# Main products in uninterrupted runs, and the rotary swap by transfers, in a hybrid decoder step on one core

## The chip, the cores and the metric

The kernel runs on one core of one Trainium2 chip. The metric is the device time of one execution in microseconds. A core has five engines with an instruction stream each: TensorE (PE), VectorE (DVE), ScalarE (ACT), GpSimd (POOL) and SyncE (SP, which issues the transfers here). Every stream is worked off in the order in which it was written when the program was built; where an instruction waits, those behind it on the same engine wait too.

## The reference

One decoder layer works on a prompt of 1024 positions and on 8 single-token samples; the kernel puts the 1032 columns side by side. Cut to the prompt's mixer and the rest of the layer:

```python
qkv, z, xbc, dt_raw = split_mix(rmsnorm(x) @ w_in)
for g, (window, dil) in enumerate(((128, 1), (512, 4), (2048, 16))):
    q, k, v = rope(qkv[g, 0]), rope(qkv[g, 1]), qkv[g, 2]       # 8 heads x 64
    o[g], lse[g] = dilated_window_prompt(q, k, v, dil)           # 128 keys back
attn = sum(softmax(lse)[g] * o[g] for g in range(3))
y, h_new = ssd_chunked(*conv_silu(xbc, dt_raw))                  # 16 heads, chunks of 128
ssm = rmsnorm(y * silu(z))
h = x + rmsnorm(concat(attn, ssm) @ w_out)
out = h + rmsnorm((silu(gate) * up) @ w_ffn_out)                 # gate, up of rmsnorm(h) @ w_ffn_in
```

`rope` rotates the two halves of a head against each other: `x1*cos - x2*sin` and `x2*cos + x1*sin`. All results are f32. The samples read caches of keys and values and write them back shifted by one position.

## The kernel before

**Main products.** Activations lie with features on the 128 partitions and the 1032 positions along the free axis. Each operand of a large product is split into a high and a low part (`wh`/`wl`, `xh`/`xl`), and three of the four products are formed. `unit` (line 167 on, the product itself at line 175) computes a block of 128 output features by a third of the positions (344 columns): 8 blocks of the inner dimension, 3 products each, so 24 products into one PSUM bank. `gemm` loads a weight block (`load_w`) and calls `unit` for the three thirds, each followed by an eviction. Such products are called main products here.

**What runs beside them.** The input projection goes first through the 12 blocks that the SSD branch needs, then through 12 blocks for each of three attention patterns (per head pair one for v, q, k: `do_v`, `do_qk`, then `attend`), then through the 8 blocks of `z`. Side work fills in: the SSD chunks (`ssd`, tiles `xt`, `gb`, `yp`, `yo`, `stp`), the rotation (`do_qk`) and the attention (`attend`). `attend` takes a head pair through 8 rounds j: scores `sps` (for two rounds at once, line 646), mask and maximum by DVE into `sm` (L652), `ngm` (L656), exponential by ACT (L660), transposes `ptp` (L667), a copy to `pt` by DVE or ACT (L671, L673), and the product with v, `nps` (L680). `vtp` (L604) are the transposes of v. `ptp` and `vtp` share a pool of one PSUM bank, which is handed out in program order; `qrp`, `krp`, `vtp` (SBUF), `rawp` and `swpp` have two buffers each.

**Rotation.** `do_qk` gets `rw`, the raw projection, from ACT's evictions (L586). Four ACT copies of 32 partitions (L615) write the halves exchanged into `sw`, POOL multiplies `sw` by the sines (L616), DVE `rw` by the cosines (L617), and DVE adds both into `qr` (L620).

**The merge.** When all three patterns are done, their maxima and sums are stored and read back (`st_d`, `sn`), weights are formed (`wo`, transposed as `wtp`, L842) and 16 steps follow (L850 to L859): load `nt` and the weights `wt`, POOL multiplies (L855), DVE adds twice (L856, L857), ACT and DVE split the sum into `ah` and `al`. There are two buffers of `nt`. The output projection takes the SSD part first (`sh`/`sl`, evicted by DVE into `mix`, L239) and the attention part (`ah`/`al`, weights `wah`/`wal`, L980 and L981) after. Then comes the FFN.

**What sets the order.** A scheduler with a model of the engines puts the instructions into their streams when the program is built. Of those that its model has ready it takes the one with the lowest priority number. `prio(kind)` (line 55) sets that number from one running counter for each kind (line 52): evictions from 1 million, weights from 5, side work from 10, the merge (`late`) from 20, main products from 50. So a main product goes where nothing else is ready. The tables and buffers of the rotation are given back behind the third pattern (`rope.close()`), and the buffers of `z` (`zt`) and of the gate (`yg`) come to lie where they were.

## Time and profile before

| | us |
|---|---|
| median of 3 runs | 1859.24 (1858.23 to 1863.11) |
| profiled execution | 1865.26 |
| its span, first to last instruction | 1863.5 |
| PE busy (matmuls) | 1776.0 (95% of the span) |
| DVE busy | 1141.2 |
| ACT busy | 781.4 |
| POOL busy | 320.0 |

Busy is the union of the times in which an engine works. Matmuls overlap in the pipeline, so a busy PE need not be one at its peak; how far apart the products start tells more. The mean granted TensorE clock is 0.98 of full speed. The span has four parts: the SSD inputs (to about 215 us), the three attention patterns with SSD chunks beside them (to 885 us), the `z` products with the merge (to 1050 us), and the output projection and FFN.

### The profile page before, as it was taken

To read this page: it belongs to the slowest core of one execution; us is meant where nothing else is said; L and a number is where in the kernel's file an instruction comes from. 1 tells how busy PE (TensorE), PEld (TensorE's weight loads), DVE (VectorE), ACT (ScalarE), POOL (GpSimd) and SP (SyncE) were. 2 spreads that over 40 slices of the span, in tenths; PEclk is the share of its full clock that TensorE was granted. 3 is DMA by queue.
4 is the path that set the end of the run, shared out by engine and by line. 5 is a ranking of instruction groups with operands and counts; after the bars stand their busy time and mean duration, and the time that the engine had idled before them with its cause. 6 is when DMAs were issued, how large, how long until landed. Compare 5 with 4: busy or idle time off the path is not lost.

```text
span 1863.5 us, 30669 instructions
## 1 busy us (share of the span) xinstructions
PE 1776.0 (95%) x12183; PEld 1659.1 (89%) x12183; DVE 1141.2 (61%) x2228; ACT 781.4 (42%) x1433; POOL 320.0 (17%) x218
## 2 busy tenths in 40 slices
PE   8999999999998999999878999999999999999995
PEld 6999877888887889988758999999999999999995
DVE  6545666766765454446667499886666666423338
ACT  5533554455554555556333235532222222431133
POOL 0000245444234221123442301000000000000020
PEclk9999999999999999999988999999999999999998
DMA  4322344434334243346566355355545445976686
GB/s 157 135 100 79 97 127 125 128 121 116 114 103 156 90 137 103 123 152 224 171 167 182 101 160 180 110 199 171 176 151 183 167 151 197 351 264 215 207 314 206
DMA packets 135198, 298.59 MB, mean 160 GB/s; under 512 B 18432, under 2 KB 85600, under 8 KB 133648
## 3 DMA queue, kind: packets, MB, share of 16 engines
q1 hardware_dynamic: 135056, 296.64, 48.4%
q8 instruction: 95, 1.56, 0.3%
q14 instruction: 47, 0.39, 0.1%
HBM read 247.49 MB, written 137.10 MB: 206 GB/s over the span
## 4 chain that ended last, share of the span: by engine, by line
PE 37%; DVE 8%; DMA 3%; issue 1%; ACT 1%; POOL 1%; DVEq 0%; SPq 0%; POOLq 0%; ACTq 0%
PE fb L1217 20%; PE g L175 16%; DMA nt<-n_d 1%; PE g L955 1%; DVE xr L1043 1%; POOL nt L855 1%; DVE fl L1058 1%; DVE nacc L1000 1%; DVE mix L1055 0%; DVE nt L856 0%; DVE fac L1341 0%; DMA wr<-in_w_fin 0%; DVE nt L857 0%; DMA out_yT<-fac 0%; DMA wt<-w_d 0%
## 5 line engine op out<-in xcount | busy, mean ns | idle before, releaser
L175 PE MATMUL g<-xh,wh 128*128 128x344 f32 x1344 | 443.6, 330 | 9.3 <-ACT zt L903 5.1
L175 PE MATMUL g<-xl,wh 128*128 128x344 f32 x1344 | 440.3, 328 | 1.5 <-DVE xl L231 1.5
L175 PE MATMUL g<-xh,wl 128*128 128x344 f32 x1344 | 439.2, 327 | 0.5 <-DVE wl L164 0.5
L175 PEld LDWEIGHTS g<-xh,wh 128*128 128x128 f32 x1344 | 255.6, 190 | 19.0 <-ACT zt L903 5.6
L175 PEld LDWEIGHTS g<-xh,wl 128*128 128x128 f32 x1344 | 256.2, 191 | 12.3 <-issue 11.0
L175 PEld LDWEIGHTS g<-xl,wh 128*128 128x128 f32 x1344 | 256.1, 191 | 10.6 <-issue 7.7
L1217 PE MATMUL fb<-fh,wsl 128*128 128x258 f32 x1216 | 222.5, 283 | 0.1
L1217 PEld LDWEIGHTS fb<-fh,wsl 128*128 128x128 f32 x1216 | 188.0, 189 | 0.4 <-DVE fs L1113 0.3
L1217 PE MATMUL fb<-fl,wsl 128*128 128x258 f32 x608 | 171.9, 283 | 0.0
L164 DVE TENSOR_TENSOR wl<-wr,wh 128x1024 fp32r<-128x1024 f32 (+1 forms) x93 | 111.7, 1202 | 80.2 <-ACT wh L163 79.9
L175 PE MATMUL g<-hh,wh 128*128 128x344 f32 x432 | 138.1, 320 | 0.1
L175 PE MATMUL g<-hh,wl 128*128 128x344 f32 x432 | 137.8, 319 | 0.0
L175 PE MATMUL g<-hl,wh 128*128 128x344 f32 x432 | 136.9, 320 | 0.0
L163 ACT CAST wh<-wr 128x1024 fp32r<-128x1024 f32 (+1 forms) x93 | 92.5, 995 | 95.0 <-PE g L175 91.5
L660 ACT ACTIVATE sm<-sm,ngm 128x128 f32<-128x128 f32 (+1 forms) x192 | 84.9, 443 | 106.1 <-DVE ngm L656 102.2
L1300 POOL TENSOR_TENSOR ow<-wr,ow 128x512 fp32r<-128x512 f32 x8 | 10.9, 1395 | 658.8 <-ACT ow L1299 658.8
L616 POOL TENSOR_TENSOR sw<-sw,sin 128x1032 f32<-128x1032 f32 x24 | 72.8, 3032 | 251.0 <-ACT sw L615 187.6
L1217 PEld LDWEIGHTS fb<-fl,wsl 128*128 128x128 f32 x608 | 114.9, 189 | 0.0
L615 ACT COPY sw<-rw 32x1032 f32<-32x1032 f32 x96 | 101.0, 1052 | 1.4
L586 ACT COPY rw<-g 128x344 f32<-128x344 f32 x108 | 47.2, 443 | 111.8 <-PE g L175 71.5
L1221 DVE TENSOR_TENSOR fo<-fp,fb 128x258 f32<-128x258 f32 x152 | 62.8, 420 | 45.4 <-PE fb L1217 43.3
L175 PEld LDWEIGHTS g<-hh,wh 128*128 128x128 f32 x432 | 81.2, 188 | 0.3 <-ACT fac L1284 0.3
(362 smaller groups left out, 3801.2 us busy)
## 6 DMA issues: line engine op xcount, KB each, us to landing
out_skv<-in_cache SPq DMA_DIRECT2D x64, 1023.5 KB, 5.7
wr<-in_w_in SPq DMA_DIRECT2D x56, 512.0 KB, 3.7
out_skv<-in_cache SPq DMA_DIRECT2D x16, 1022.0 KB, 5.6
wr<-in_w_out SPq DMA_DIRECT2D x24, 512.0 KB, 3.7
hr<-hid_d SPq DMA_DIRECT2D x22, 516.0 KB, 6.2
hid_d<-fo SPq DMA_DIRECT2D x38, 258.0 KB, 4.5
wg<-in_w_fin SPq DMA_DIRECT2D x19, 512.0 KB, 4.2
wu<-in_w_fin SPq DMA_DIRECT2D x19, 512.0 KB, 5.1
```

The source lines that it names most:

```text
L163: nc.scalar.copy(wh[:, :cols], wr[:, :cols])
L164: nc.vector.tensor_tensor(out=wl[:, :cols], in0=wr[:, :cols], in1=wh[:, :cols], op=ALU.subtract)
L175: last = nc.tensor.matmul(ps, x[:, ws], y[:, c0:c1], start=(k == 0 and j == 0), stop=(k == n - 1 and j == 2))
L586: return nc.scalar.copy(rw[:, c0:c1], ps)
L615: nc.scalar.copy(sw[q * 32:(q + 1) * 32, 0:T], rw[s * 32:(s + 1) * 32, :])
L616: nc.gpsimd.tensor_tensor(out=sw[:, 0:T], in0=sw[:, 0:T], in1=sin, op=ALU.mult)
L660: nc.scalar.activation(out=sm[:, h, :nk], in_=sm[:, h, :nk], func=AF.Exp, scale=SCALE, bias=ngm[:, g, j, i:i + 1], accum_out=den[:, g, j, ...
L855: nc.gpsimd.tensor_tensor(out=nt, in0=nt, in1=wt, op=ALU.mult)
L955: nc.tensor.matmul(pq[m][c], ws[m][j == 1][:, k * P:(k + 1) * P], (sl if j == 2 else sh)[k][:, CH[c][0]:CH[c][1]], start=(k == 0 and j == ...
L1000: nc.vector.tensor_tensor(out=acc, in0=acc, in1=sq, op=ALU.add)
L1217: nc.tensor.matmul(ps, x[:, ks], y, start=(k == 0 and j == 0), stop=(k == 3 and j == 2))
L1221: return nc.vector.tensor_tensor(out=dst, in0=x, in1=y, op=ALU.add)
```

## The change

A main product gets the priority `main` only where it is the first of a run; the others get the new kind `run`, whose numbers (from 3 million) come before weights and side work. A run has 12 products until the second pattern begins and 24, a whole unit, from then on. In `do_qk` the four copies that exchange the halves become four transfers issued by SP, and the multiplication by the sines goes from POOL to DVE. In `attend` all copies to `pt` are made by ACT.

```diff
--- before.py
+++ after.py
@@ -49,7 +49,7 @@
 
 def trunk(tc, a, o):
     nc = tc.nc
-    ctr = {"evac": 1_000_000, "w": 5_000_000, "side": 10_000_000, "late": 20_000_000, "main": 50_000_000}
+    ctr = {"evac": 1_000_000, "run": 3_000_000, "w": 5_000_000, "side": 10_000_000, "late": 20_000_000, "main": 50_000_000}
 
     @contextmanager
     def prio(kind):
@@ -164,14 +164,17 @@
                 nc.vector.tensor_tensor(out=wl[:, :cols], in0=wr[:, :cols], in1=wh[:, :cols], op=ALU.subtract)
         return wh, wl
 
+    run = [12]
+
     def unit(ps, w, hs, ls, c, ch=CH):
         wh, wl = w
         c0, c1 = ch[c]
         n = len(hs)
-        with prio("main"):
-            for k in range(n):
-                ws = slice(k * P, (k + 1) * P)
-                for j, (x, y) in enumerate(((wh, hs[k]), (wl, hs[k]), (wh, ls[k]))):
+        for k in range(n):
+            ws = slice(k * P, (k + 1) * P)
+            for j, (x, y) in enumerate(((wh, hs[k]), (wl, hs[k]), (wh, ls[k]))):
+
+                with prio("main" if (3 * k + j) % run[0] == 0 else "run"):
                     last = nc.tensor.matmul(ps, x[:, ws], y[:, c0:c1], start=(k == 0 and j == 0),
                                             stop=(k == n - 1 and j == 2))
         return last
@@ -612,8 +615,8 @@
             sw = swpp.tile([P, 3 + T], F32, tag="swp", name="sw")
             for q in range(4):
                 s = q ^ 1
-                nc.scalar.copy(sw[q * 32:(q + 1) * 32, 0:T], rw[s * 32:(s + 1) * 32, :])
-            nc.gpsimd.tensor_tensor(out=sw[:, 0:T], in0=sw[:, 0:T], in1=sin, op=ALU.mult)
+                nc.sync.dma_start(out=sw[q * 32:(q + 1) * 32, 0:T], in_=rw[s * 32:(s + 1) * 32, :])
+            nc.vector.tensor_tensor(out=sw[:, 0:T], in0=sw[:, 0:T], in1=sin, op=ALU.mult)
             nc.vector.tensor_tensor(out=rw, in0=rw, in1=cos, op=ALU.mult)
             qp = krp if which else qrp
             qr = qp.tile([P, S], F32, tag="qr", name="qr")
@@ -667,10 +670,7 @@
                     nc.tensor.transpose(tp[:, q * P:(q + 1) * P], sm[:, h, b * P:(b + 1) * P], ident)
             pt = ptp.tile([P, 4, P], F32, tag="pt", name="pt")
             dst = pt[:, 0:2 * nb].rearrange("p q t -> p (q t)")
-            if j % 2 and j % 4 < 2:
-                nc.scalar.copy(dst, tp[:, :2 * nk])
-            else:
-                nc.vector.tensor_copy(dst, tp[:, :2 * nk])
+            nc.scalar.copy(dst, tp[:, :2 * nk])
             if j % 4 == 0:
                 nps = att_ps("nps")
 
@@ -758,6 +758,7 @@
 
     with prio("side"):
         dec_scores(0)
+    run[0] = 24
     pattern(1)
     with prio("side"):
         dec_scores(1)
```

**PE behind main product 3648.** The main products are counted along PE's stream; this is the end of the eighth unit of `z`. Before, this stood there (`g` is a main product, `pnp` belongs to the samples):

```order
L175 MATMUL g<-xh_119,wl 128x344
L787 MATMUL pnp<-ident,pn_8388 128x32
L787 MATMUL pnp<-ident,pn_8391 128x32
L787 MATMUL pnp<-ident,pn_8394 128x32
L792 MATMUL pnp<-ident,sal 128x32 x2
L680 MATMUL nps<-pt,vt 64x128 x2
L667 MATMUL ptp<-ident,sm 128x128 x2
L646 MATMUL sps<-qr 128x128 x4
L792 MATMUL pnp<-ident,sal 128x32 x4
L175 MATMUL g<-xl_127,wh 128x344
```

Now 29 rows stand there between one main product and the next, with eight groups of `ptp`; these are the ones in the middle:

```order
L680 MATMUL nps<-pt,vt 64x128 x2
L670 MATMUL ptp<-ident,sm 128x128 x2
L649 MATMUL sps<-qr 128x128 x4
L680 MATMUL nps<-pt,vt 64x128 x2
L607 MATMUL vtp<-ident,vp 128x128 x4
L788 MATMUL pnp<-ident,pn_8388 128x32
L788 MATMUL pnp<-ident,pn_8391 128x32
L788 MATMUL pnp<-ident,pn_8394 128x32
L793 MATMUL pnp<-ident,sal 128x32 x6
L607 MATMUL vtp<-ident,vp 128x128 x4
L670 MATMUL ptp<-ident,sm 128x128 x2
L680 MATMUL nps<-pt,vt 64x128 x2
```

Rounds of the third and the fourth head pair, and the transposes of the fourth pair's v, moved here; they stood between main products 3428 and 3640 before.

**SP in the third pattern.** Before, SP issued there the weight loads (`wr`), the outputs of the rotated keys (`out_pk2`) and of v (`out_pv2`), and cache copies (`out_skv`), each of which waits for an eviction:

```order
L148 DMA wr_7866<-in_w_in 128x1024
L627 DMA out_pk2<-qr_7297 128x1024
L690 DMA n_d_339<-nh_6871 128x1024
L129 DMA out_skv0<-in_cache0 16x8128
L594 DMA out_pv2<-rw_7435 128x1024
L148 DMA wr_7969<-in_w_in 128x1024
L129 DMA out_skv0<-in_cache0 16x8128
L148 DMA wr_8065<-in_w_in 128x1024
```

Now the pieces of the swap (`sw`) stand among them, for q and k of the third head pair:

```order
L690 DMA n_d_339<-nh_6871 128x1024
L148 DMA wr_8751<-in_w_in 128x1024
L618 DMA sw_7624<-rw_7538 32x1032 x4
L618 DMA sw_7720<-rw_7634 32x1032 x2
L129 DMA out_skv1<-in_cache1 16x16352
L618 DMA sw_7720<-rw_7634 32x1032 x2
L597 DMA out_pv2<-rw_7865 128x1024
L148 DMA wr_8841<-in_w_in 128x1024
```

One cache copy came to stand between the two halves of a swap.

**DVE at the end of the merge.** `nt_8614` and `nt_8624` are the last two of the 16 steps, `mix4` to `mix7` the output blocks whose SSD part DVE evicts. Before:

```order
L239 TENSOR_TENSOR mix4_9531<-g_9773,rt_8748 128x344
L856 TENSOR_TENSOR nt_8614<-nt_8614 128x256
L857 TENSOR_TENSOR nt_8614<-nt_8614 128x256
L859 TENSOR_TENSOR al_8436<-nt_8614,ah_8435 128x256
L239 TENSOR_TENSOR mix4_9531<-g_9799,rt_8748 128x344
L856 TENSOR_TENSOR nt_8624<-nt_8624 128x256
L164 TENSOR_TENSOR wl_9885<-wr_9883,wh_9884 128x1024
L857 TENSOR_TENSOR nt_8624<-nt_8624 128x256
L859 TENSOR_TENSOR al_8436<-nt_8624,ah_8435 128x256
L239 TENSOR_TENSOR mix5_9532<-g_9831,rt_8748 128x344
```

Now:

```order
L857 TENSOR_TENSOR nt_8614<-nt_8614 128x256
L858 TENSOR_TENSOR nt_8614<-nt_8614 128x256
L242 TENSOR_TENSOR mix6_9533<-g_9889,rt_8748 128x344
L860 TENSOR_TENSOR al_8436<-nt_8614,ah_8435 128x256
L857 TENSOR_TENSOR nt_8624<-nt_8624 128x256
L858 TENSOR_TENSOR nt_8624<-nt_8624 128x256
L860 TENSOR_TENSOR al_8436<-nt_8624,ah_8435 128x256
L242 TENSOR_TENSOR mix6_9533<-g_9915,rt_8748 128x344
L242 TENSOR_TENSOR mix7_9534<-g_9947,rt_8748 128x344
```

The last steps moved back by about one and a half output blocks of 48 main products each.

## Rows read from the trace of the kernel before

**Rows 1.** Busy time by stage: window, us, engines busy (instructions), PE clock, DMA share, GB/s.
```profile
215.00:590.00 375.00, 361.55 (x2553) 308.31 (x2552) 254.03 (x597) 198.39 (x411) 151.31 (x107) 0.99 0.39 119
...
885.00:1050.00 165.00, 141.04 (x772) 125.03 (x771) 108.82 (x137) 54.88 (x79) 64.26 (x38) 0.92 0.59 162
1050.00:1863.50 813.50, 787.35 (x5714) 782.71 (x5712) 514.69 (x910) 266.87 (x425) 26.12 (x14) 0.98 0.58 198
```

**Rows 2.** Waits of PE, 215 to 700 us: who, for whom, us, times, longest.
```profile
PE sps L646 <- DVE qr L620: 10.7, 4, 5.4
PE xt L497 <- DMA xg<-xs_d: 7.7, 4, 2.4
PE g L175 <- ACT rw L586: 3.5, 6, 1.3
```

**Rows 3.** Time line of PE around one visit: start us, us, instruction, count.
```profile
308.09 0.31 PE L175 MATMUL g<-xh,wl 128*128 128x344 f32 x1
308.33 0.66 PE L680 MATMUL nps<-pt,vt 128*64 128x128 f32 x8
308.92 0.66 PE L667 MATMUL ptp<-ident,sm 128*128 128x128 f32 x4
309.33 0.41 PE L175 MATMUL g<-xl,wh 128*128 128x344 f32 x1
309.57 0.33 PE L175 MATMUL g<-xh,wh 128*128 128x344 f32 x1
309.74 0.32 PE L175 MATMUL g<-xh,wl 128*128 128x344 f32 x1
```

**Rows 4.** The same around the last round of attention.
```profile
889.57 0.44 PE L680 MATMUL nps<-pt,vt 128*64 128x128 f32 x4
889.93 0.44 PE L667 MATMUL ptp<-ident,sm 128*128 128x128 f32 x2
```

**Rows 5.** Groups by line, 215 to 885 us: busy us, mean ns, idle before it.
```profile
L615 ACT COPY sw<-rw 32x1032 f32<-32x1032 f32 x92 | 96.8, 1052 | 1.4
L616 POOL TENSOR_TENSOR sw<-sw,sin 128x1032 f32<-128x1032 f32 x23 | 70.4, 3059 | 195.6 <-ACT sw L615 132.2 <-PE ptp L667 25.4 <-PE g L175 24.7
...
L652 DVE CUSTOM_DVE_ANT_0 sm<-sps,mask 128x128 f32<-128x128 f32 (+1 forms) x192 | 59.4, 357 | 34.9 <-PE ptp L667 26.3 <-PE sps L646 8.0 <-ACT nh L688 0.3
...
L617 DVE TENSOR_TENSOR rw<-rw,cos 128x1032 f32<-128x1032 f32 x23 | 37.4, 1627 | 18.6 <-ACT sw L615 18.6
```

**Rows 6.** DMA issues, 215 to 880 us: count, KB each, median us to landing.
```profile
out_pv<-rw SPq DMA_DIRECT2D x4, 512.0 KB, 5.8
...
out_pv<-rw SPq DMA_DIRECT2D x3, 64.0 KB, 1.6
```

**Rows 7.** Time line of ACT in a round of the third pattern.
```profile
876.93 0.40 ACT L660 ACTIVATE sm<-sm,ngm 128x128 f32<-128x128 f32 x1
...
877.62 0.19 ACT L660 ACTIVATION_READ_ACCUMULATOR sm<-sm,ngm 128x1 f32 x1
880.44 0.37 ACT L671 COPY pt<-ptp 128x256 f32<-128x256 f32 x1 [2.63 <-PE ptp L667]
```

**Rows 8.** Busy time by stage, a stretch in which PE waits.
```profile
970.00:980.00 10.00, 6.33 (x19) 5.16 (x20) 7.22 (x7) 6.26 (x9) 4.87 (x3) 0.58 0.43 107
```

**Rows 9.** POOL's merge multiply, L855: idle before it (us, times), until what.
```profile
  DMA nt<-n_d: 51.8, 9
```

**Rows 10.** Tile `ah`: duration ns min/median/max, first and last start.
```profile
L175 PE MATMUL g<-ah,wah x48: 314/320/323, 1051.1 to 1128.0; 128*128 128x344 f32 x48
...
L859 DVE TENSOR_TENSOR al<-nt,ah x16: 410/422/1900, 935.8 to 1035.9; 128x256 fp32r<-128x256 f32 x16
```

**Rows 11.** Tile `wah`: the split of the attention part's weights.
```profile
L981 POOL TENSOR_TENSOR wal<-wr,wah x2: 2421/2428/2434, 1040.0 to 1047.2; 128x1024 fp32r<-128x1024 f32 x2
```

**Rows 12.** Waits of SP's queue, 215 to 880 us: us, times, longest.
```profile
SPq L148 <- DVE wl L164: 96.0, 23, 17.8
SPq L129 <- ACT rw L586: 77.1, 10, 13.8
```

## The prediction, made before the changed kernel ran

> **What bounds the kernel now.** The table above has PE busy for 95% of the span, but a share over the whole span says little, so I read the busy times by stage first [rows 1]. From 1050 us to the end (output projection and FFN) PE is busy 787 of 813 us, and nothing in the change is aimed there. From 215 to 590 us (the first two attention patterns beside the SSD chunks) it is busy 362 of 375 us. From 885 to 1050 us, where the patterns are merged beside the `z` products, it loses most: 141 of 165 us at a granted clock of 0.92. So there are two questions: do products and attention pass PE faster or slower before 885 us, and does the end of attention, from which the merge starts, come earlier or later? Second, the waits of PE between 215 and 700 us [rows 2] name three things worth having: scores that wait for the rotated `qr` (10.7 us), SSD transposes that wait for a load (7.7 us), and products that wait for an eviction by ACT (3.5 us). Third, PE's time line around one visit to attention work [rows 3] gives the price that the regrouping is to save.
>
> **Part 1: fewer visits.** Counted in the order up to the first FFN product of the blocked kind (`fb`), main products stand in 212 uninterrupted runs before and in 133 now, nearly all of 12, 24 or 48, so 79 visits to side work go. One visit costs, by [rows 3]: the step from a product to `nps` takes 0.24 us (308.09 to 308.33) where one product follows another after about 0.16, so 0.08 going in; the first product after it takes 0.24 again (309.33 to 309.57), 0.08 coming out; `ptp` to product adds nothing to the 0.41 us of the four transposes. That is 0.16 x 79 = 13 us saved. But the side work is the same and now stands in longer pieces: changes from one kind of side product straight to another rise from 220 to 288. Eight `nps` take 0.59 us until `ptp` starts [rows 3], four take 0.36 [rows 4]: 0.06 for each, so 0.12 is the change, and 68 x 0.12 = 8 us are given back. With changes to and from `sps`, which no row here isolates, it may be twice that. The net lies between -6 and +4 us; I take -3. The regrouping as such is nearly free of gain: what goes at the border between products and side work comes back between the kinds of side work.
>
> **Part 2: the rotary swap.** 96 ACT copies of 1.05 us go (92 of them in this stretch, 96.8 us), and so do 24 POOL multiplies of 3.06 us. DVE takes the multiply, at the price of its twin with the cosines, 1.63 us [rows 5], and gives its 72 `pt` copies to ACT. For each tile the chain from `rw` to the sum was 4 x 1.05 + 3.06 = 7.3 us and becomes a transfer plus 1.6 us. No transfer from SBUF to SBUF stands in the trace. The nearest rows write SBUF to memory: 64 KB of `rw` land 1.6 us after issue, 512 KB after 5.8 [rows 6]. A piece here is 129 KB, and four are issued in turn, so 2.5 to 7 us; I take 3.3, near the 64 KB row. The chain is then 4.9 us, 2.4 shorter (bounds: 3.2 shorter, 1.3 longer). ACT and POOL hold up PE in this stretch only through `qr` and `rw`, so their relief is worth at most what PE waited for those two, 14.2 us, and with the loads 21.9 [rows 2]. Of the four `qr` waits about 7 us go if each shortens by 2.4; with a little for the other two I take 9 us saved, bounds 0 and 20.
>
> **Part 3: attention falls behind the products.** The order shows this, the short description doesn't. A run once started outranks side work, so side work gets one gap per 24 products, where the 212 runs before left one per about 13 in this stretch, and a gap carries mostly one round of attention. A pattern has 36 units and 32 rounds, and the `vtp` and scores need gaps too, so attention just fails to keep up. In the order the scores of the last head pair first appear behind product 3648 instead of 3520, and the last `nps` of attention behind 3816 instead of 3736. Those 80 products, 0.16 us each, are done before the end of attention instead of behind it: +12.8 us for that end.
>
> The lag has a second price. At product 3648 the `z` products must stop, since their buffers lie where `rawp`, `swpp` and the tables lay, and those are free only when the last `vtp` has read `vp`; `vtp` shares one PSUM bank with `ptp` in program order, so it stands behind every round of the third head pair. Where two pieces of side work stood there, 8 rounds stand now, with `vtp` in their middle and no product between them; behind product 3288 there are four. With the smaller places, 11 more rounds than before have no product beside them. What does such a round cost? PE's own work in it I put at 0.9 us: 0.36 for `nps`, 0.2 for two transposes, and half a group of scores. ACT cannot do a round faster than two exponentials (876.93 to 877.81) and a copy of 0.37, 1.25 us [rows 7]; a round with nothing overlapped adds two masks on DVE of 0.36 us [rows 5] and PE's 0.9, some 3 us. So PE idles 0.35 to 2.1 us for each round; as two can overlap I take 1.1, 12 us in all. Add 3 us (0 to 6) for an SSD chain that now stands alone behind product 2280, and 3 us (0 to 6) of slow clock: +18 us, bounds 4 and 35.
>
> On the clock: from 970 to 980 us, where PE waits for side chains, the granted clock is 0.58, a mix of 2.4 and 1.2 GHz [rows 8], against 0.99 from 215 to 590 us with its many short visits [rows 1]. The Trainium skill (TensorE: Matmul & The Clock Gate, section Loop structure matters more than you think) says that a loop nest which keeps the products dense keeps the clock up, and that long waits between them lose it; the trace agrees, with its 0.58. By that rule longer runs help; by [rows 1] the clock before 590 us leaves them 1% to win, and the stretch behind 3648 is one of the kind that loses it.
>
> **Part 4: the merge.** It is a chain of 16 steps, whose `nt` loads wait for one of two buffers; POOL waits 51.8 us for them [rows 9]. It starts from the end of attention and ends with the `al` that starts at 1035.9; the first product on `ah` starts at 1051.1 [rows 10]. Behind the chain only a weight load and its split are needed: `wal` starts at 1040.0 and takes 2.4 us [rows 11], so 1042.4 would do, which leaves 8.6 us of slack. In DVE's order six SSD evictions stood between the chain's end and the products on `ah`, worth the 15 us from 1035.9 to 1051.1; now there are three, about 7.5 us, hardly more than the 6.5 that load and split take. The slack is used up, so the first product on `ah` moves by what the end of attention moves, less 8.6 us. Bounds: all of it (0), or 25 us less, if transfers and DVE are freer because more products are done already.
>
> **The sum**, against the profiled execution's own 1865.26 us: +12.8 (products ahead) - 3 (visits) + 18 (rounds alone) - 9 (shorter waits) = +18.8 at the end of attention; - 8.6 (slack) = +10.2 at the first product on `ah`. From there both programs are bound by PE, and it stays. The profiled execution lies 6.0 us above the median of 1859.24; on the median I forecast 1869 us. What a measurement of this kernel can tell from no change is 0.3%, 5.6 us.
>
> **Rivals.**
> *Longer runs pay (faster).* The place is the stretch from 215 to 885 us. If rounds alone overlap down to ACT's pace (5 us in all), the visits save their most and nearly all waits of [rows 2] go, the end of attention moves by 12.8 - 6 + 5 - 20 = -8; less the slack's 8.6 and with 2 us of clock lost that is -15, so 1844 us. For it: ACT loses up to 74 us of work (101 less 72 x 0.37), POOL 73, and the waits of [rows 2] are real. It decides where a round alone leaves PE idle for less than 0.5 us. Against it: the swap's transfers start from SP's queue.
> *SP's queue holds the swap (much slower).* SP works in order, and it stood still for weight buffers 96.0 us in 23 times, up to 17.8, and behind cache copies that wait for an eviction 77.1 us in 10, up to 13.8 [rows 12]. A swap behind such a row makes `qr` late, and PE waits in front of `sps`. In the third pattern a cache copy stands between two halves of a swap. Two such waits of 10 us over the forecast: 1889 us. Against it: a weight load and the swap of an earlier tile become ready at nearly the same time.
> *It comes out even.* The copies and multiplies that go lay beside PE, the runs were 13 long already, and the slack of the merge takes the lag: 12.8 - 3 + 10 - 12 - 8.6 = -1, so 1858 us.
>
> **How the numbers follow.** The forecast has 0.42, the held swap 0.12, even 0.20, faster 0.26. Slower by over 0.3%: 0.12 and all but 0.02 of the 0.42, so 0.52. Faster by over 0.3%: 0.26 and 0.01 of the even case's spread, 0.27; no change 0.21. The range is 1842 to 1896 us: it holds the faster case and the held swap, and leaves out that several bounds meet, as a merge 25 us quicker with all waits gone, or 35 us of rounds alone behind a held swap. The forecast's own range is 1858 to 1882.
>
> **What would show it.** Right: one stretch of 15 to 20 us between 860 and 910 us in which no main product runs, PE waits in front of `ptp`, `nps` and `vtp`, and the clock falls; few waits for `qr` before 700 us; `wtp` 15 to 25 us later; the first product on `ah` near 1061 us. Wrong: that stretch with PE busy throughout; products before 590 us clearly denser than 0.16 us; `sps` that waits for `sw` transfers over 5 us a time; or a merge over in much less than its 100 us.

## The result, and the profile of the changed kernel

The changed kernel is slower: 1905.07 us median of 4 runs (1904.16 to 1914.37), against 1861.17 us for the kernel before beside it. The ratio is 1.0231, with a 95% interval of 1.0201 to 1.0260. The direction was forecast; the size, +10, was not: it is +44 us on the medians, and the time lies outside the range. The profiled execution took 1914.37 us with a span of 1912.6, 49.1 over the span before, so the sums below are a few us larger than the medians say.

The stages of the changed kernel (window, us, busy time of PE, PEld, DVE, ACT and POOL with their instructions, granted clock, DMA share, GB/s) answer to [rows 1]:

```profile
215.00:590.00 375.00, 352.43 (x2389) 302.91 (x2388) 225.89 (x534) 149.81 (x365) 106.62 (x86) 0.95 0.43 127
...
885.00:1050.00 165.00, 139.39 (x776) 117.76 (x776) 103.88 (x183) 76.21 (x144) 63.56 (x37) 0.88 0.57 172
1050.00:1912.60 862.60, 824.86 (x5917) 817.86 (x5915) 536.52 (x942) 275.53 (x438) 43.13 (x23) 0.98 0.58 195
```

The first two of these rows have a lower clock than before (0.95 for 0.99, 0.88 for 0.92), and everything behind them is late. The waits of PE from 215 to 700 us (us, times, longest), against [rows 2]:

```profile
PE g L178 <- ACT rw L589: 16.9, 9, 3.7
PE xt L500 <- DMA xg<-xs_d: 6.6, 2, 4.1
PE sps L649 <- DVE mx L655: 3.6, 2, 2.8
PE nps L680 <- ACT pt L673: 2.1, 4, 0.7
```

The waits for `qr` are gone, as forecast. A new one stands in their place: a main product that waits for ACT to evict `rw`, 16.9 us where it was 3.5. From 700 us to the last `nps` of attention the changed kernel has these, and the one before, up to its own last `nps` at 894 us, the two behind:

```profile
PE stp L754 <- DVE scs L750: 6.5, 1, 6.5
PE nps L680 <- ACT pt L673: 6.3, 9, 1.6
PE sps L649 <- DVE mx L655: 4.0, 5, 1.5
```
```profile
PE stp L754 <- DVE scs L750: 1.1, 1, 1.1
PE pnp L787 <- DVE pn L786: 1.1, 1, 1.1
```

Behind main product 3648 the changed kernel does what the order said, but for 32 us (891.3 to 923.9 without a main product). The time line of PE there (start, us, instruction, count, idle before it):

```profile
891.27 0.31 PE L178 MATMUL g<-xl,wh 128*128 128x344 f32 x1
...
892.25 0.72 PE L649 MATMUL sps<-qr 64*128 64x128 f32 x8
894.37 0.44 PE L680 MATMUL nps<-pt,vt 128*64 128x128 f32 x4 [1.41 <-ACT pt L673]
894.74 0.44 PE L670 MATMUL ptp<-ident,sm 128*128 128x128 f32 x2
901.68 0.61 PE L754 MATMUL stp<-ident,scs 128*32 128x128 f32 x2 [6.50 <-DVE scs L750]
```

and the same place by windows, then the kernel before over its own last rounds of attention:

```profile
889.00:896.40 7.40, 4.77 (x37) 3.62 (x35) 4.67 (x9) 2.78 (x8) 3.25 (x2) 1.00 0.53 182
896.40:927.10 30.70, 20.86 (x95) 14.36 (x96) 13.56 (x59) 14.70 (x49) 5.17 (x4) 0.50 0.49 183
927.10:940.00 12.90, 12.90 (x89) 11.85 (x88) 8.85 (x12) 9.30 (x15) 6.72 (x5) 1.00 0.58 193
```
```profile
860.00:894.00 34.00, 32.93 (x217) 29.21 (x218) 22.38 (x59) 21.38 (x47) 9.54 (x6) 0.95 0.53 182
```

For 30.7 us the granted clock is 0.50, the lower level of 1.2 GHz, in one piece. It comes back only where main products run again, 3.2 us after the first of them. It fell at 896.4, 1.2 us after the long wait for `scs` had begun. Before, rounds of attention lay between main products, at 0.95, with PE busy 97%.

The later stations, against [rows 10] and [rows 11]:

```profile
L178 PE MATMUL g<-ah,wah x48: 313/320/488, 1093.0 to 1174.9; 128*128 128x344 f32 x48
...
L860 DVE TENSOR_TENSOR al<-nt,ah x16: 360/424/1858, 991.7 to 1091.4; 128x256 fp32r<-128x256 f32 x16
```
```profile
L982 POOL TENSOR_TENSOR wal<-wr,wah x2: 2340/2370/2400, 1091.9 to 1094.3; 128x1024 fp32r<-128x1024 f32 x2
```

The merge still takes 100 us (991.7 to 1091.4) and starts 55.9 later; the first product on `ah` comes 41.9 later (1093.0 for 1051.1).

### The profile page after: what moved, and what is told of

It reads as the page before. It is cut to its first block, busy times and chain, and to the rows that moved or that the text cites. A ratio compares the mean times of both kernels' runs of the same rounds, so it can differ in the third digit from the quotient of the medians.

```text
span 1912.6 us, 30770 instructions
## 1 busy us (share of the span) xinstructions
PE 1799.8 (94%) x12183; PEld 1680.1 (88%) x12183; DVE 1109.2 (58%) x2180; ACT 709.9 (37%) x1411; POOL 250.8 (13%) x194
## 5 line engine op out<-in xcount | busy, mean ns | idle before, releaser
L178 PE MATMUL g<-xh,wh 128*128 128x344 f32 x1344 | 450.9, 336 | 22.2 <-ACT rw L589 16.9
L178 PEld LDWEIGHTS g<-xh,wh 128*128 128x128 f32 x1344 | 259.5, 193 | 41.8 <-ACT rw L589 20.7
L178 PEld LDWEIGHTS g<-xh,wl 128*128 128x128 f32 x1344 | 260.1, 194 | 1.6 <-DVE wl L164 0.8
L655 DVE CUSTOM_DVE_ANT_0 sm<-sps,mask 128x128 f32<-128x128 f32 (+1 forms) x192 | 59.9, 347 | 83.1 <-PE ptp L670 48.5
L1301 POOL TENSOR_TENSOR ow<-wr,ow 128x512 fp32r<-128x512 f32 x8 | 10.1, 1291 | 657.6 <-ACT ow L1300 657.6
L1222 DVE TENSOR_TENSOR fo<-fp,fb 128x258 f32<-128x258 f32 x152 | 63.0, 421 | 49.1 <-PE fb L1218 45.2
L178 PEld LDWEIGHTS g<-hh,wl 128*128 128x128 f32 x432 | 81.2, 188 | 0.0
```

Of the source, the lines that this page charges most:

```text
L178: last = nc.tensor.matmul(ps, x[:, ws], y[:, c0:c1], start=(k == 0 and j == 0), stop=(k == n - 1 and j == 2))
L655: nc.vector.tensor_tensor_reduce(out=sm[:, h, :nk], in0=sps[h][:, c0:c0 + nk], in1=msk, scale=1.0, scalar=0.0, op0=ALU.add, op1=ALU.max, a ...
L1222: return nc.vector.tensor_tensor(out=dst, in0=x, in1=y, op=ALU.add)
L1301: nc.gpsimd.tensor_tensor(out=wl, in0=src, in1=wh, op=ALU.subtract)
```

## The experiments

Times are medians beside runs of the kernel before on the same chip. "Behind" is ratio less 1, times the median before (1861 to 1866 us). The stations come from each kernel's profile: the last `nps` of attention, the main products started by then, the time at half clock up to then, the last `al`, the first product on `ah`. Two traces of one order differ too: up to product 3600 the order on PE of one kernel below (`e18_nostp`) is that of the changed kernel, and its profile reaches that product 7.6 us earlier. Differences of stations between kernels are good to some 8 us.

| kernel | ratio (95%) | behind, us | last `nps` | products | half clock | last `al` | first on `ah` |
|---|---|---|---|---|---|---|---|
| before | 1 | 0 | 894.1 | 3736 | 23.9 | 1035.9 | 1051.1 |
| runs (e1) | 1.0253 (1.0234 to 1.0271) | +47 | 936.2 | 3792 | 71.7 | 1080.4 | 1095.8 |
| swap (e2) | 1.0049 (1.0033 to 1.0066) | +9 | 912.0 | 3781 | 30.7 | 1050.4 | 1058.6 |
| pt (e3) | 1.0127 (1.0108 to 1.0147) | +24 | 910.2 | 3812 | 20.5 | 1054.1 | 1068.7 |
| runs, pt (e4) | 1.0359 (1.0339 to 1.0379) | +67 | 977.3 | 3864 | 109.2 | 1114.9 | 1116.5 |
| swap, pt (e5) | 1.0032 (1.0018 to 1.0047) | +6 | 899.0 | 3736 | 23.9 | 1041.2 | 1056.3 |
| runs, swap (e11) | 1.0195 (1.0169 to 1.0220) | +36 | 923.3 | 3792 | 54.6 | 1068.0 | 1083.1 |
| all three (changed) | 1.0231 (1.0201 to 1.0260) | +43 | 955.9 | 3816 | 92.2 | 1091.4 | 1093.0 |
| runs, patterns 1 and 2 (e9) | 1.0000 (0.9985 to 1.0015) | 0 | 909.3 | 3794 | 27.3 | 1043.8 | 1047.2 |
| runs of 12 throughout (e8) | 1.0158 (1.0126 to 1.0189) | +29 | 935.5 | 3828 | 64.9 | 1074.2 | 1075.8 |
| runs from 2784 on (e12) | 1.0171 (1.0147 to 1.0195) | +32 | 918.3 | 3792 | 44.4 | 1066.4 | 1081.5 |
| runs up to 3216 (e13) | 1.0190 (1.0167 to 1.0212) | +35 | 926.6 | 3806 | 51.2 | 1066.4 | 1080.5 |

### The three edits, alone and together

**Runs alone**, `e1_runs`: before, with the new kind and `run` only.

```
-        with prio("main"):
-            for k in range(n):
+        for k in range(n):
...
+                with prio("main" if (3 * k + j) % run[0] == 0 else "run"):
...
+    run[0] = 24
     pattern(1)
```


> Only the grouping of main products is changed (runs of 12 in the first pattern, 24 from the second on); the rotary swap and the pt copies are those of before. Its trace has the place behind main product 3648 at which nothing but side work stands (6 rounds, 19 pieces; after: 8 and 25; before: none).
> Theory R (the runs are the loss: attention falls behind, and what then stands alone runs at half clock): most of after's loss comes back, +25 to +45 us, 1886 to 1906 us; a stretch of 15 to 30 us at half clock near 890 us.
> Theory S (the swap by transfer is the loss: DVE, in order, waits for it, and ACT's evictions wait behind): between -5 and +10 us, 1856 to 1871 us, with a short piece at half clock near 890 us.
> The rival 'longer runs pay' as put in the prediction: -10 us or better.

Measured: 1911.50 us (1908.14 to 1914.37). Theory R, a little above its range.

**Swap alone**, `e2_swap`:

```
-                nc.scalar.copy(sw[q * 32:(q + 1) * 32, 0:T], rw[s * 32:(s + 1) * 32, :])
-            nc.gpsimd.tensor_tensor(out=sw[:, 0:T], in0=sw[:, 0:T], in1=sin, op=ALU.mult)
+                nc.sync.dma_start(out=sw[q * 32:(q + 1) * 32, 0:T], in_=rw[s * 32:(s + 1) * 32, :])
+            nc.vector.tensor_tensor(out=sw[:, 0:T], in0=sw[:, 0:T], in1=sin, op=ALU.mult)
```


> Only the rotary swap is changed: four transfers from SP's queue in place of ACT's four copies, the multiply by the sines on DVE in place of POOL. Main products lie as before (209 runs up to the first blocked product, 212 before).
> Theory S: DVE waits for sw some 60 us in all as in after, the cache copies' evictions behind it make PE wait; +15 to +35 us, 1876 to 1896 us.
> Theory R: the swap costs little or gains the few us that I had put on it: -9 to +6 us, 1852 to 1867 us, although DVE waits, since PE has enough other work.
> Theory P (the pt copies on ACT are the loss): as R here.

Measured: 1873.56 us (1868.70 to 1878.82), between the two theories.

**pt alone**, `e3_pt`: the branch goes and `nc.scalar.copy(dst, tp[:, :2 * nk])` stays.

> Only the pt copies are changed: all on ACT, where before a quarter were. ACT keeps the 96 swap copies too, so it has 72 more copies of 0.37 us, 27 us of work, and DVE is freed of as much.
> Theory P (pt in ACT's order, behind exponentials and evictions that wait, is a good part of the loss): +10 to +25 us, 1871 to 1886 us, PE waits for pt in front of nps over 10 us in all.
> Theories R and S: within 5 us of before, 1856 to 1866 us, since ACT has room.

Measured: 1889.06 us (1883.61 to 1890.38): nearly Theory P's number (3 us above its range), for a part to which the prediction had given no term. But Theory P's mechanism is not there. It wanted over 10 us of waits for `pt`, and the trace up to the last `nps` has

```profile
PE nps L677 <- ACT pt L670: 2.0, 1, 2.0
```

All waits of PE from 215 us up to there grow only from 28.3 to 34.0 us. What grows is the number of main products ahead of the end of attention: 3812, 76 more than before. At the 0.157 us from one main product to the next these are 12 of the 16.1 us by which attention ends later; the last `al` and the first product on `ah` come 18 us later. That the order is the cause is read from these counts; no run tests it alone.

**Runs and pt**, `e4_noswap`: the changed kernel with ACT's copies and POOL's multiply put back.

> The change without its swap: runs of 12 and 24 and all pt copies on ACT; ACT swaps and POOL multiplies as before. Behind main product 3648 eight rounds stand alone, behind 3072 and 3288 four and three.
> Theory S: close to before, -5 to +12 us (1856 to 1873 us): the loss goes with the swap.
> Theory R: close to after, +30 to +45 us (1891 to 1906 us).
> If the two add up, each about half: +15 to +25 us.

Measured: 1930.05 us (1929.00 to 1935.78). Neither theory has it: without the swap the changed kernel would be 24 us slower still. **Swap and pt**, `e5_noruns`, put `with prio("main")` back around the unit:

> The change without its runs: swap by transfers with the sines on DVE, all pt copies on ACT, main products in the order of before. Alone the swap cost 10 us and the pt copies 26.
> Theory A (ACT's order is what pt fills and the swap empties: each edit undoes the other): +5 to +12 us, 1868 to 1876 us, so that the runs alone make up the rest of after's 43.9.
> Theory B (the two add up, and only the runs make the swap pay): +30 to +38 us, 1893 to 1902 us.

Measured: 1871.47 us (1869.23 to 1876.99). Theory A: beside each other the two cost 6 us, less than either alone. **Runs and swap**, `e11_nopt`, put the branch of the copies back:

> The change without its pt copies: runs of 12 and 24, swap by transfers with the sines on DVE, three quarters of the pt copies on DVE as before. Behind main product 3648 seven rounds stand alone, behind 3072 four.
> Theory A (the runs are worth some 48 us, and swap and pt cancel as far as ACT's order is concerned): without pt the swap's own 10 us come on top of the runs, +45 to +60 us, 1908 to 1924 us.
> Theory B (with the runs in place the swap saves 22 us, as it does beside pt): +22 to +32 us, 1885 to 1896 us.

Measured: 1902.26 us (1898.81 to 1905.09), a little above Theory B. In the three kernels with runs and another edit the loss of the runs shows; swap and pt move it by -11 to +20.

### Where the runs lose

**Runs in the first two patterns only**, `e9_runs_p01`: e1 with one line more.

```
+    run[0] = 1
     pattern(2)
```


> Only the grouping, and only in the first two patterns (12, then 24); in the third the products stand as before, one at a time. No place behind 3648 where side work stands alone.
> Theory L (the loss is what the lag makes at the end: the rounds alone behind 3072 and 3648, their waits and their half clock): 0 to +12 us, 1863 to 1876 us, since main products of the first two patterns passed no later at product 2448 (+2 us) in the run with runs throughout.
> Theory D (long runs lose all along, by the waits at their ends and the clock that falls behind them): +20 to +35 us, 1884 to 1899 us.

Measured: 1866.30 us (1860.45 to 1868.74), before beside it 1866.37: the low end of Theory L. 212 uninterrupted runs became 173 up to the first `fb`, with nothing won and nothing lost. Its largest wait of PE from 215 to 700 us is the new one, longer than in the changed kernel although the swap is the old one:

```profile
PE g L178 <- ACT rw L589: 24.5, 10, 7.7
```

So it is the runs that bring this wait (a unit reaches its PSUM bank before ACT has evicted it), in exchange for those of [rows 2], 21.9 us. **Runs of 12 throughout**, `e8_runs12`, are e1 without `run[0] = 24`:

> Only the grouping, runs of 12 throughout (no step to 24). Behind 3648 five rounds stand alone (6 with 24), behind 3072 none (4 with 24).
> Theory L: the stretch behind 3072 does not come (worth 14 us in the run with 24) and that behind 3648 stays: +20 to +36 us, 1884 to 1900 us.
> Theory 24 (the step to 24 is the whole loss): within 8 us of before, 1856 to 1872 us.
> Theory D: as with 24, less a few us, +38 to +46 us.

Measured: 1895.21 us (1892.43 to 1898.91). Theory L. **Runs of 24 from product 2784 on**, `e12_third`, count the products in `unit`:

```
+        run = 24 if m0 >= 2784 else 1
```


> Only the grouping, and only from main product 2784 on, the third pattern and the z products (runs of 24); the first two patterns as before. Behind 3648 the same 6 rounds stand alone as with runs throughout, behind 3072 none.
> Theory L (what stands alone behind 3648 and what follows from it is the loss): +24 to +36 us, 1888 to 1900 us, like runs of 12 throughout, which have that place too.
> Theory C (the loss needs the long runs of all three patterns, their lag added up): within 10 us of before, 1856 to 1876 us.

Measured: 1895.88 us (1895.00 to 1899.94). Theory L: the third pattern alone is enough, with no lag from the first two. **Runs of 12 and 24 up to product 3216**, `e13_catch`:

```
+        run = 12 if m0 < 1920 else 24 if m0 < 3216 else 1
```


> Only the grouping: runs of 12, of 24 from product 1920 on, and from 3216 on, two thirds through the third pattern, one product at a time as before, so that attention catches up. Five rounds stand alone behind 3072, none behind 3648.
> Theory L: the loss behind 3648 (21 to 26 us in the runs that have it) is gone, that behind 3072 (about 14 us) stays but the slack behind attention's end takes it: 0 to +14 us, 1863 to 1878 us.
> Theory D' (long runs lose wherever they stand in the third pattern): half of the 47 us, +20 to +28 us, 1884 to 1892 us.

Measured: 1899.94 us (1899.01 to 1901.85). A miss for Theory L and worse than Theory D'. There is no place alone behind 3648, and still attention ends 32.5 us later than before, with 70 products more ahead of it. Its five rounds behind product 3072 look like those behind 3648 in small:

```profile
735.00:754.00 19.00, 16.06 (x122) 13.19 (x120) 5.21 (x24) 9.30 (x17) 0.00 (x0) 1.00 0.30 88
754.00:764.20 10.20, 7.10 (x30) 5.07 (x31) 5.88 (x16) 7.39 (x20) 3.42 (x1) 0.50 0.01 2
```

Product 3168 comes 12.6 us later than before, 3744 19.4, 4032 17.8 and 4320 29.5. So bunched rounds cost wherever in the third pattern they stand, and no slack took it up.

**The change with the third pattern as before**, `e14_third1`: the same line as in e9, put into the changed kernel.

> The change with one line more: from the third pattern on one product at a time, as before. Runs of 12 and 24 in the first two, swap by transfers, sines on DVE, pt copies on ACT. No place behind 3648.
> Theory L: the runs cost nothing then; what is left is the +6 us of swap and pt together: 0 to +8 us, 1863 to 1872 us.
> Theory S (the swap's waits on DVE cost by themselves beside the runs): +15 to +25 us.

Measured: 1881.54 us (1879.03 to 1884.60), ratio 1.0090 (1.0069 to 1.0111), +17. The line takes 26 us off the changed kernel. The 17 left are Theory S's number and more than e9 and e5 together (6), so there is a second loss, for which the third pattern's runs are not needed. Where the two lie shows in the starts of main products, in us later than before:

| kernel | 2880 | 3600 | 3648 | 3744 | last `nps` |
|---|---|---|---|---|---|
| runs (e1) | 2.2 | 8.2 | 26.2 | 30.9 | 42.1 |
| runs, patterns 1 and 2 (e9) | 7.1 | 8.1 | 3.5 | 4.1 | 15.2 |
| all three (changed) | 21.4 | 22.0 | 47.6 | 47.9 | 61.8 |
| the same, third pattern as before (e14) | 16.8 | 18.2 | 16.0 | 15.7 | 19.7 |

Of the changed kernel's 47.9 us at product 3744, 21.4 are there at product 2880, ahead of any place with rounds alone in the third pattern, and 25.6 come between 3600 and 3648, where e14 has none. Up to product 2880 the changed kernel has 54.6 us at half clock, e14 44.4, the kernel before 20.5. The early loss stands where runs and pt come together: at product 2880 e4 (runs, pt) is 15.8 us late, e5 (swap, pt) 5.3, and e11 (runs, swap) 8.2 early. With e4 late and no transfer in it, the swap's waits, Theory S's reason, can't be needed for it; what does it is not shown. **A candidate**, `e15_p01_swap`: e9 with the swap by transfers, its multiply left on POOL.

> A candidate: runs of 12 and 24 in the first two patterns only, swap by transfers, but the multiply by the sines stays on POOL and the pt copies stay as before. The last transposes of attention stand behind product 3706 (before 3713, the runs in two patterns alone 3771).
> If it is the multiply on DVE (in order, waiting for the transfer) that made the swap cost 10 us alone: -12 to -3 us, 1851 to 1860 us. If the transfers themselves cost: +4 to +10 us, 1867 to 1873 us.

Measured: 1906.96 us (1903.02 to 1909.54), ratio 1.0224 (1.0202 to 1.0246), +42: outside both. An early end of attention in the order (3706) is worth nothing if PE cannot run the order: 20 us are lost between products 2448 and 2592, and `nps` waits 18.3 us for `pt` up to the end of attention. Those copies stand in DVE's order behind decode sums that wait for POOL (40.0 us in all, up to 9.7) and behind cosines that wait until the transfers have read `rw` (40.3, up to 5.8).

### What slows the rounds that stand alone

**No wait for the decode scores**, `e18_nostp`: the changed kernel with

```
-            nc.tensor.transpose(stp[:32, h * P:(h + 1) * P], scs[:, h]..., ident)
+            nc.tensor.transpose(stp[:32, h * P:(h + 1) * P], ident[:, 0:32] if g == 2 else scs[:, h]..., ident)
```


> The changed kernel, but the last two transposes of decode scores read the identity in place of the scores, so that they wait for nothing (what is left out: the decode scores of the third pattern). In the changed kernel PE waits 6.5 us there, and from that wait on the clock is at half for 30.7 us, over 12 rounds or parts of rounds with PE busy 73 to 83%.
> Theory W (the wait brings the clock down, and the side work behind it runs at half speed for that reason): the stretch keeps full clock or loses it for under 10 us; 6.5 us of wait and about 8 of clock come back, -10 to -18 us against after, 1887 to 1896 us.
> Theory T (rounds without main products are too thin for full clock): the clock falls all the same, for 20 us or more; -2 to -7 us, 1898 to 1903 us.

Measured: 1902.49 us (1897.79 to 1904.47), ratio 1.0209 (1.0192 to 1.0226). By the time Theory T; but the edit did not do what it was for. A wait for another decode tile came in its place, and the clock fell within that one (at 891.9; the wait ended at 892.2), for 27.3 us:

```profile
PE pnp L788 <- DVE pn L787: 4.6, 1, 4.6
```

**Four transposes for one**, `e20_dup`, on top of it:

```
+                    for _ in range(4 if g == 2 and hp >= 2 else 1):
```


> As e18_nostp, and each transpose of the exponentials in the last two head pairs of the third pattern is issued four times (same data, same place): 96 more than needed in 16 rounds and 0.1 us each at full clock, some 10 us more work for PE.
> Theory T (the clock follows how dense PE's work is in the rounds): less time at half clock behind 3648 than in e18_nostp, by 10 us or more, and the time the same as there or up to 5 us less although PE has 10 us more to do.
> Theory W, or a clock that does not respond: the extra work shows, +4 to +12 us against e18_nostp.

Measured: 1910.51 us (1907.51 to 1917.00), 8 us over e18, as the clock that does not respond would have it. Here the wait for `pn` shrank to 0.4 us. The waits of PE from 884 to 927 us, and windows around the stretch at half clock:

```profile
PE sps L649 <- DVE mx L655: 3.1, 3, 2.1
PE nps L681 <- ACT pt L674: 1.4, 2, 0.8
```
```profile
892.00:899.10 7.10, 5.91 (x42) 5.22 (x42) 4.35 (x20) 3.54 (x13) 2.58 (x2) 1.00 0.34 104
899.10:926.40 27.30, 24.43 (x113) 18.61 (x113) 13.09 (x38) 11.29 (x34) 5.77 (x6) 0.50 0.74 266
926.40:937.00 10.60, 10.60 (x74) 9.81 (x73) 5.93 (x14) 8.63 (x17) 3.43 (x3) 1.00 0.18 63
```

The longest wait there is 2.1 us, and that at 887; the clock fell all the same, for 27.3 us, and PE is busy 89% of it, at half speed. So it takes no long wait, which speaks against Theory W, and making PE's work denser with transposes did not hold the clock, against what Theory T expected. It is one profile, but the changed kernel has a smaller place of the kind: behind product 3288 four rounds stand alone, and the clock falls at 821.3 for 6.8 us with no wait over 0.7 us before it. In `e6_pool` it falls 0.2 us ahead of a wait of 3.9 us, and in the six others with a long stretch within a wait of 4.4 to 6.5 us. In e12 the stretch at half clock behind 3648 is 23.9 us; in e9, where main products lie between the rounds, there is none:

```profile
865.50:889.40 23.90, 19.09 (x83) 13.46 (x84) 12.46 (x51) 12.45 (x41) 7.47 (x5) 0.50 0.68 249
```
```profile
893.00:912.00 19.00, 19.00 (x128) 17.46 (x127) 11.84 (x24) 10.48 (x20) 9.55 (x6) 1.00 0.40 118
```

One kernel departs from this. In e11, with seven rounds alone behind 3648, the clock came back between two pieces, 10.7 us before the next main product, and fell again:

```profile
870.40:880.60 10.20, 7.55 (x38) 4.71 (x37) 5.47 (x17) 4.14 (x16) 5.18 (x5) 0.50 0.65 196
880.60:884.10 3.50, 0.80 (x5) 0.31 (x3) 0.69 (x1) 0.58 (x1) 1.70 (x2) 0.99 0.96 306
884.10:894.30 10.20, 7.76 (x35) 5.65 (x35) 7.49 (x27) 5.94 (x18) 2.17 (x2) 0.50 0.94 365
```

What brings the clock down in such a stretch, and what brings it back, stays open.

### What the swap costs

`e10_swap_pool` is e2 with the multiply left on POOL, `e6_pool` the changed kernel with the same.

> The kernel before with only the copies of the swap turned into transfers; the multiply by the sines stays on POOL, so DVE has no more to do than before. With the multiply on DVE the swap cost 10 us alone.
> Theory DVE (the multiply waits for the transfer in DVE's order and holds what is behind it): within 4 us of before, 1859 to 1868 us.
> Theory transfer (four issues on SP and a landing of 2.3 to 7.5 us make qr late in any case): +8 to +20 us, 1871 to 1884 us, since the multiply on POOL is slower by 1.8 us.

> The changed kernel, but the multiply by the sines stays on POOL.
> Theory DVE: -5 to -12 us against after, 1893 to 1900 us.
> Theory transfer: +2 to +15 us against after, 1907 to 1920 us.

Measured: 1887.72 us (1884.15 to 1891.96), ratio 1.0127 (1.0104 to 1.0150), +24; and 1907.22 us (1904.62 to 1912.27), 1.0234 (1.0212 to 1.0256), no different from the changed kernel and at the low end of Theory transfer. In e10 Theory DVE is refuted: alone, the multiply on DVE is the good half of the edit (e2 loses 9 us, e10 24), the transfer the bad one. Beside runs and pt it makes no difference where the multiply stands. Its chain by tile, from the start of the first piece to the start of the sum, is 8.1 us (median of 24) before, 9.3 in e2, 10.1 in the changed kernel and 10.4 in e10. Issues of the changed kernel (count, KB, median us to landing), and its multiplies of 215 to 885 us (busy us, mean ns, idle before):

```profile
sw<-rw SPq DMA_DIRECT2D x96, 129.0 KB, 2.5
```
```profile
L619 DVE TENSOR_TENSOR sw<-sw,sin 128x1032 f32<-128x1032 f32 x23 | 28.4, 1235 | 66.8 <-DMA sw<-rw 63.8 <-DMA kt<-in_cache 2.3 <-DMA y_d<-xg 0.8
```

## Why the prediction was wrong, step by step

I set every step of PE from one product's start to the next, from 215 us to the last `nps`, against the median of the same pair at full clock in the trace before. What is over by more than 0.45 us I count as a wait, the rest as clock if the clock was at half, and otherwise as visits. Against the trace before, in us:

| term | forecast | runs alone (e1) | changed kernel |
|---|---|---|---|
| work ahead of attention's end at full clock (main products) | +12.8 | +12.0 | +17.6 |
| visits | -3 | -5.7 | -7.0 |
| waits (rounds alone 12, SSD chain 3, shorter waits -9) | +6 | +22.8 | +28.4 |
| slow clock | +3 | +14.0 | +23.5 |
| end of attention | +18.8 | +42.1 | +61.8 |
| slack of the merge | -8.6 | +2.6 | -19.9 |
| behind the first product on `ah` | 0 | +4.4 | +7.1 |
| span | +10.2 | +49.1 | +49.1 |

The columns leave under 1.5 us open. How much goes to which row depends on which steps count as the same pair: by tile or by tile and shape, slow clock in the changed kernel comes out between 22 and 27 us and waits between 28 and 33. By count alone the main products are 80 x 0.157 = 12.6 us there and 56 x 0.157 = 8.8 in e1, less than the first row has. So the rows give sizes, not single us; the table of product starts above needs no pairing.

**Part 1, visits: right in kind.** Gone are 79 visits, and they are worth little; the -7.0 lies just beyond the bound of -6. e9 shows a kernel with 39 fewer visits and no time won.

**Part 3, the lag: mechanism right, two sizes wrong.** The 80 products are there (3816 for 3736). The term that failed here is "3 us (0 to 6) of slow clock": it is some 23.5. The prediction named the stretch behind 3648 as one of the kind that loses the clock, but gave the 3 us no working. Time at half clock up to the last `nps` is 92.2 us where it was 23.9; the stretch behind 3648 has 30.7 of it, and 34.1 of the 68.3 more lie ahead of product 2880, where the sum had 3 us for an SSD chain and otherwise only gains. And the price of a round alone, 2.0 us from PE's 0.9 plus 1.1 idle, was taken at full clock: from `nps` to the next transposes PE takes 0.37 us at full clock and 0.63 at half. The waits of the lag were sized well: 12 and 3 forecast, and the profile's rows from 700 us on grow from 3.6 to 21.2 us in all.

That the stretch would stand alone only behind 3648 and 3288 was right; that the long decode chain ends in it was not seen: each of 8 steps loads, multiplies on POOL and sums on DVE, and `stp` waits 6.5 us for the last. What this wait is worth by itself is not shown, since in e18 another of 4.6 us took its place.

**Part 2, the swap and the waits: wrong in sign.** The term "9 (shorter waits)" failed, and with it "I take 3.3, near the 64 KB row": the four issues take some 0.6 us each on SP, and a piece lands 2.5 us after its issue, so the fastest multiply starts 4.2 us after the first issue, and the median one 5.9 to 7.2. The chain became longer by 1 to 2 us, not 2.4 shorter. Hence DVE waits for `sw`, with everything behind it in its order:

```profile
DVE sw L619 <- DMA sw<-rw: 66.6, 21, 12.7
```

The -9 for shorter waits is +6.5 by the rows of 215 to 700 us (24.7 before, 31.2 after, all groups), since the runs put the wait for `rw` where those for `qr` stood; with the clock, PE is 21.4 us late at product 2880. What I had not seen is that the swap is worth something else in company: alone it costs 9 us, but beside runs and pt it saves 24 (e4 to the changed kernel), beside pt 18, beside the runs 11. That its worth changes with the other edits is shown. That ACT's load is the reason is argued, and it can't be all, for the runs give ACT nothing more to do.

The pt copies got no term in the sum and cost 24 us alone, by the counts mostly through the order that the scheduler then chose.

**Part 4, the slack: right in kind, read from the wrong rows.** The 15 us between the last `al` and the first product on `ah` were not DVE's six evictions but the second weight pair. `wah` is made twice, and I had taken only the first: `wal` at 1040.0 and 2.4 us behind it, where [rows 11] have a second at 1047.2. From its end to the first product on `ah` are 1.5 us, not 8.6. Before, the first of three loads of the row below is issued at 1035.1 and the second pair's at 1042.5, when the split of the first has ended and given a load buffer back; its own split ends at 1049.6. In the changed kernel both are issued by 1081, ahead of the last `al`, and only the splits are left:

```profile
L978 SPq DMA_DIRECT2D wr<-in_w_out x3: 367/368/368, 1035.1 to 1043.5; - x3
```
```profile
L979 SPq DMA_DIRECT2D wr<-in_w_out x2: 378/489/600, 1074.4 to 1080.6; - x2
```

From the last `al` to the first product on `ah` are 15.2 us before, 1.6 in the changed kernel, 3.4 in e9 and 15.4 in e1. Where the second pair comes early, the first product on `ah` moves 17 to 20 us less than attention's end (e8, e4, e9, the changed kernel): e9 ends attention 15 us later and loses nothing. In the changed kernel part of it is given back: the second split ends 3.6 us after the first product on `ah`, PE waits 2.9 us for it, and 5.4 of the 7.1 us behind that product arise within the next 80 main products.

Of the rivals, "longer runs pay" is refuted by the result, and in e9, where the runs stand without the stretch, they pay nothing. "It comes out even" falls with the result too. "SP's queue holds the swap" is not the main thing, for the runs lose 47 us without the swap. Of the signs that were to prove the forecast, the stretch of 15 to 20 us without main products was 32, and `wtp`, expected 15 to 25 us later, came 62.8 later (974.9 for 912.1). The direction was right, but a good part of the loss came from places for which the prediction had a gain.

What stays open: why runs and pt together lose 16 to 21 us up to product 2880 (e4, e14, the changed kernel), why e13 loses 35 (12.6 by product 3168 with the bunched rounds, and 70 products ahead of attention's end are 11 by count), and why e15 loses 42. Their losses are located, their causes only in part.

## What to carry to other kernels

Side work that is kept waiting is not saved up for free: where it must be done before the next main products can start, it runs alone, and here mostly at half clock; price a round that would stand alone with PE's part at that clock (0.63 us where 0.37 stood). Look for the buffers or banks at which the main stream must stop, and count what side work stands in front of that point before and after a change of priority. And price an edit that moves work between engines in the company it will have: the swap was +9 us alone and -24 beside two other edits.

## What the runs showed of the hardware that was not expected

Nine of these kernels have five to eight rounds of side work alone behind 3648. In eight of them the granted clock fell to 0.50 there, for 23.9 to 30.7 us in one piece, and rose 0.3 to 6.2 us after main products came back; in e11 it did so in two pieces of 10.2 us with 3.5 us at full clock between them. With PE busy 89% of the stretch, and 96 more transposes in it and near it (e20), it stayed at 0.50. The Trainium skill (TensorE: Matmul & The Clock Gate, section Loop structure matters more than you think) has the bad case as a long wait between products; the trace agrees where there is such a wait (6.5 us in the changed kernel, and the clock falls within it), but e20 loses the clock with none over 2.1 us.

A transfer of 32 partitions from SBUF to SBUF, 129 KB, landed 2.5 us after its issue, less than the 5.6 us of the 512 KB that go to memory. DVE's multiply by the sines took 1.24 us, not the 1.63 of its twin in the kernel before, and the twin (L620) took 1.23 too. Before, 18 of the 24 twins took 1.22 to 1.24 us and six 1.57 to 3.45, so the mean in [rows 5] was not the price of the operation alone; what held the six is not tested.
